# Joining the two directions of a block-wise triangular inversion in one thread, with products that alternate between tiles of the array

## Chip, cores and metric

One NeuronCore of a Trainium2 chip runs the whole program. The metric is the device time of one execution in microseconds (us); lower is better. The time before is 1053.76 us, the median of three runs.

## The reference, cut to what matters

The reference runs two networks one after the other on 256 tokens of width 1024: a first block (a gated delta rule mixer, a layer norm, a mixture of experts with 32 experts, a gate on an embedding) and a second block of two layers. The change touches the mixer alone. Its core solves a unit lower triangular system per head and chunk:

```python
def _gated_delta_rule(q, k, v, beta, g):
    ...
    lhs = eye + jnp.einsum("nbhik,nbhjk->nbhij", kb, k) * decay * (1.0 - eye)
    solve = functools.partial(lax.linalg.triangular_solve, left_side=True, lower=True,
                              unit_diagonal=True)
    u = solve(lhs, v * beta[..., None])
    w = solve(lhs, kb * jnp.exp(gc)[..., None])
    ...
```

The mixer runs it forwards and backwards over the tokens, for 16 value heads. The kernel works with chunks of 128 tokens and inverts the 128x128 matrices: 2 directions x 16 heads x 2 chunks = 64 of them, in two batches of 32.

## The kernel before, in words

The program is written by a planner. Every piece of work is a Python generator (a thread) that yields the engine it wants next ("pe", "act", "dve"), a Wait for events, or an Alloc of buffers. `Sched.run` takes the thread that could start first by an estimate of every engine's clock, with priorities between near ones, and emits its instructions up to its next yield. So the order on each engine is fixed when the program is built, from the prices of `Sched.price` and `Sched.mm` (line 202); on the chip each engine runs its own list in order and semaphores between engines hold back what is not ready. The price of a matmul also depends on a model of the array's clock in `Sched.array` (line 215).

The first stage (class `Gdn`) projects the tokens to queries and keys (`g_qk`), values (`g_v`) and gates (`g_z`), and at its end projects the result back (`g_out`). Weights come in slabs over SP's queue; each slab is either split by ScalarE and VectorE into two parts, for which three fp32r matmuls do, or used as it is in fp32. The projections are in `Gdn.main` (line 1377), at the lowest priority (9): they fill PE wherever the threads of the heads leave room.

The inversion works on two batches `bt` of 32 matrices, each 16 per direction `d`:

- `base` (line 1164) gathers the 32x32 diagonal blocks of the batch, inverts them column by column on VectorE (`columns`, line 1207), transposes the result with two VectorE instructions into `A` and `B`, sets `base_ev`, copies the blocks to the diagonals of `Sm` and `Tm` and sets `diag_ev`.
- `lev` (line 1225) puts larger blocks together. Below, **level 1** is its first group of products (32x32 blocks of the matrix `la` times the small inverses, written to PSUM bank `px`), **level 2** the second (two products per block and matrix, from `Tm` and the small inverse, into banks `pt` and `pS`); they join 32 to 64. **Level 3** (64x64 blocks of `la` times `Tm`) and **level 4** (`Tm` times `Sm`) join 64 to 128. After each level ScalarE and VectorE copy the result from PSUM to `Tm` or `Sm`, and the next level reads it there.
- `solve` (line 1302) waits for both directions (`lev_ev`) and uses the inverses, for each of the four query/key heads of the batch.

`main` spawns `lev` twice per batch, once for each direction, so the two directions are two threads that the planner interleaves with each other and with the projections. Inside a thread, a level sends all 16 products of one pair of blocks to one tile of the array before it goes on to the other pair; where a block lies in the rows and columns is given by `span`. Only level 2 sends two products in turn, which read the same rows and write different columns. After the experts' router, the second stage loads the experts' weights into buffers that the first stage gave back.

Of the kernel before, what the change touches and what calls it, by code (L numbers as in the profile page):

```python
# [11 lines left out]
AF = mybir.ActivationFunctionType  # L12
OP = mybir.AluOpType
# [8 lines left out]
def size(ap):  # L22

    n = 1
    for d in ap.shape[1:]:
        n *= d
    return n
# [10 lines left out]
PRIO = {  # L38
    "decay": [2, 3], "pick": 4, "base": 1, "lev": 1, "solve": 7, "qk": [2, 3], "v": 5, "z": 6,
    "m_turn": 2, "ranks": 1, "gather": 4, "back": 4, "slot_w": 1, "rest": 6, "act_out": 1, "scatter": 3,  # L40
    "m_const": 2, "parts": 1, "router": 3, "norm2": 1, "e_turn": 1, "embed": 7, "e_gates": 1, "gated": 2,
    "e_const": 2, "tokens": 3, "e_head": 3, "e_conv": 3, "window": 0, "e_out": 1, "keys": 1, "normed": 2,
    "copy": 2, "o_head": 2, "o_const": 2, "select": 2, "attend": 3, "o_gate": 1, "queries": 1, "o_out": 1,
    "rms": 1, "rms_turn": 1, "project": 9, "x_split": 3,
}
# [50 lines left out]
def span(ap):  # L96

    n = 0
    for st, k in list(ap.ap)[1:]:
        n += abs(st) * (k - 1)  # L100
    o = ap.offset % max(list(ap.ap)[0][0], 1)
    return ap.name, o, o + n
# [38 lines left out]
class Sched:  # L141
# [60 lines left out]
    def mm(self, out, lhsT, rhs, first, last):  # L202
        self.nc.tensor.matmul(out, lhsT, rhs, start=first, stop=last, skip_group_check=True)  # L203
        n, m = size(rhs), size(lhsT)
        one = lhsT.dtype == F32R
        if n == 512 and m == 32:

            self.array(n, n)
            return
        self.array(max(n, 2 * m) if one else 4 * max(n, m) if n > 64 else 2.4 * n if m < 128 else max(4 * n, 2 * m),  # L210
                   (n if one else 4 * n) * rhs.shape[0] / 128.0, 0.0125 if one else 0.0025)

    TICK = 10.24 / 3
# [661 lines left out]
class Gdn:  # L875
# [346 lines left out]
                        eng.tensor_tensor(t, p2[:, k, 0:k, None].to_broadcast([128, k, n]),  # L1222
                                          R[:, k:k + 1, c:c1].to_broadcast([128, k, n]), op=OP.mult)

    def lev(self, bt, d):

        K, S = self.K, self.S
        v, s, Sm, Tm = S.v, S.s, None, None
        yield Wait(self.base_ev[bt])
        Sm, Tm = self.Sm, self.Tm  # L1230
        s32, t32 = self.AB if d == 0 else self.AB[::-1]
        u = slice(16 * d, 16 * d + 16)

        def lower(i):
            return self.LA[4 * bt + (i % 16) // 4, d][:, (i // 2) % 2, i % 2, 0]

        def span(pr):
            return 64 * pr + 32 * d, 64 * pr + 32 * (1 - d)

        px = yield Alloc("bank", [16, 32])  # L1240
        yield "pe"
        for pr in range(2):
            f, t = span(pr)
            for i in range(16 * d, 16 * d + 16):
                S.mm(px[t:t + 32, i % 16, :], lower(i)[f:f + 32, t:t + 32], t32[f:f + 32, i, :],
                     True, True)
        for pr, e in ((0, "act"), (1, "dve")):
            f, t = span(pr)
            o = Tm[t:t + 32, u, 32 * d:32 * d + 32]
            yield e  # L1250
            if pr:
                v.tensor_copy(o, px[t:t + 32])
            else:
                s.activation(o, px[t:t + 32], AF.Copy)
        S.free(px)
        yield Wait(self.diag_ev[bt])
        pt, pS = yield Alloc("bank", [16, 32], n=2)
        for pr in range(2):
            f, t = span(pr)
            yield "pe"  # L1260
            for i in range(16 * d, 16 * d + 16):
                x = Tm[t:t + 32, i, 32 * d:32 * d + 32]
                st = s32[t:t + 32, i, :]
                S.mm(pt[t:t + 32, i % 16, :], st, x, True, True)
                S.mm(pS[f:f + 32, i % 16, :], x, st, True, True)
        for pr in range(2):
            f, t = span(pr)
            yield "act"
            s.activation(Tm[t:t + 32, u, 32 * d:32 * d + 32], pt[t:t + 32], AF.Copy, scale=-1.0)
            yield "dve"  # L1270
            v.tensor_scalar(Sm[f:f + 32, u, t:t + 32], pS[f:f + 32], -1.0, None, op0=OP.mult)
        S.free(pt, pS)
        f, t = 64 * d, 64 * (1 - d)
        px = yield Alloc("bank", [8, 64], n=2)
        for half in range(2):
            yield "pe"
            for i in range(16 * d + 8 * half, 16 * d + 8 * half + 8):
                S.mm(px[half][t:t + 64, i % 8, :], lower(i)[f:f + 64, t:t + 64], Tm[f:f + 64, i, :], True, True)
        for half, e in ((0, "act"), (1, "dve")):
            o = Tm[t:t + 64, 16 * d + 8 * half:16 * d + 8 * half + 8, :]  # L1280
            yield e
            if half:
                v.tensor_copy(o, px[half][t:t + 64])
            else:
                s.activation(o, px[half][t:t + 64], AF.Copy)
            S.free(px[half])
        pS = yield Alloc("bank", [8, 64], n=2)
        for half in range(2):
            yield "pe"
            for i in range(16 * d + 8 * half, 16 * d + 8 * half + 8):  # L1290
                S.mm(pS[half][f:f + 64, i % 8, :], Tm[t:t + 64, i, :], Sm[t:t + 64, i, t:t + 64], True, True)
        for half, e in ((0, "act"), (1, "dve")):
            o = Sm[f:f + 64, 16 * d + 8 * half:16 * d + 8 * half + 8, t:t + 64]
            yield e
            if half:
                v.tensor_scalar(o, pS[half][f:f + 64], -1.0, None, op0=OP.mult)
            else:
                s.activation(o, pS[half][f:f + 64], AF.Copy, scale=-1.0)
            S.free(pS[half])
        S.set(self.lev_ev[bt][d])  # L1300

    def solve(self, bt, ml):

# [73 lines left out]
    def main(self):  # L1377
        K, S, P = self.K, self.S, self.P
        self.Sm = P.tile([128, 32, 128], F32, name="Sm")
        self.Tm = P.tile([128, 32, 64], F32, name="Tm")  # L1380
        self.V = P.tile([128, 2, 16, 128], F32, name="V")
        self.x = P.tile([128, 8, 256], F32, name="xT")
        S.spawn(self.load(), 0)
        for bt in range(2):
            S.spawn(self.base(bt), PRIO["base"])
            for d in range(2):
                S.spawn(self.lev(bt, d), PRIO["lev"])
            for ml in range(4):
                S.spawn(self.solve(bt, ml), PRIO["solve"])
        yield Wait(*self.x_ev[0:2])  # L1390
        S.spawn(self.clear(), 3)
        x = (self.xh, self.xl, self.x)
        acc = None
        for name, i in GDN_ORDER:
            if name == "g_qk":
                b = yield from K.feature_major(name, x, x_ev=self.xs_ev)
                S.spawn(self.qk_head(i, b), PRIO["qk"][i > 3])
            elif name == "g_v":
                b = yield from K.feature_major(name, x, x_ev=self.xs_ev)
                S.spawn(self.v_pair(i, b), PRIO["v"])  # L1400
            elif name == "g_z":
                if i == GDN_FULL:

                    for n, t in zip(("oh", "ol"), x[0:2]):
                        S.slot_views(n, t.rearrange("p (k a) t -> p k (a t)", a=2))
                z = yield Alloc(("z", "zx"), [512])
                b = yield from K.feature_major(name, x, True, x_ev=self.xs_ev)
                S.spawn(self.z_pair(i, b, z), PRIO["z"])
            else:
                if acc is None:  # L1410
                    acc = yield from K.acc()
                yield Wait(self.z_ev[i])
# [12 lines left out]
        self.entry.start(self.x1)  # L1425
# [1625 lines left out]
```

## Time and profile before

| what | us |
|---|---|
| median of three runs | 1053.76 (1052.91 to 1054.62) |
| the profiled execution | 1055.7 |
| its span, first to last instruction | 1053.9 |
| first inversion, level 1 to the end of level 4 | 121.2 to 158.1 |
| second inversion, the same | 274.9 to 304.9 |
| PE busy | 981.7 |
| mean granted clock of PE | 0.966 |

In a table of stretches each engine has its busy time and, in brackets, how many instructions ran; PEclk is the granted clock, where 1.00 is 2.4 GHz and 0.50 is 1.2 GHz. PEld is the weight load of a matmul. Tile names stand for what an instruction writes and reads: `bank<-t,la` is level 1, `bank<-Tm,t` and `bank<-t,Tm` level 2, `bank<-Tm,la` level 3, `bank<-Sm,Tm` level 4 (all at line 203, where the helper issues every matmul; line 126 is the helper for the other engines). An fp32 product is recorded as two loads and two matmuls.

### The profile page before, as it was taken

The numbers are of one execution on the slowest core, as the hardware profiler recorded it, in microseconds if no ns is written. First come the engines' busy times: TensorE is split into PE (matmuls) and PEld (weight loads), VectorE is DVE, ScalarE is ACT, GpSimd is POOL, SyncE is SP. The second block draws the span as 40 slices with busy tenths as digits, with TensorE's granted clock in tenths as the row PEclk, the third lists the DMA queues.
The fourth block names the chain that finished last, engine by engine and source line by source line (L and its number), as shares of the span: only waits on it lengthen the run. The fifth ranks groups of instructions, "written<-read, shape, count | busy, mean of one in ns | idle before, by whom it ended". The sixth has DMA issues, their size and how long they took to land. (4 is left out here: it accounts for less than half of the span.)

```text
span 1053.9 us, 17204 instructions
## 1 busy us (share of the span) xinstructions
PE 981.7 (93%) x6828; PEld 748.5 (71%) x6828; DVE 621.0 (59%) x1150; ACT 485.4 (46%) x896; POOL 123.6 (12%) x129
## 2 busy tenths in 40 slices
PE   8999989999899968998988779999999999998998
PEld 7788889888688762423211139899999988986886
DVE  7869856699835651121111146688776765677673
ACT  3888464893325331201000135666575443545562
POOL 2133220121000220000000043000000000004230
PEclk9999889999899959999999978999999999999999
DMA  6422411124323977999999954354544454633321
GB/s 217 141 95 86 141 61 41 62 100 136 124 83 123 411 310 288 415 416 410 417 412 414 416 187 146 126 185 160 176 146 159 153 177 172 240 113 99 120 81 41
DMA packets 56680, 205.38 MB, mean 195 GB/s; under 512 B 6416, under 2 KB 6800, under 8 KB 56208
## 3 DMA queue, kind: packets, MB, share of 16 engines
q1 hardware_dynamic: 56304, 204.02, 53.0%
q8 instruction: 55, 0.90, 0.3%
q10 hardware_dynamic: 288, 0.19, 0.1%
q14 instruction: 33, 0.27, 0.1%
HBM read 203.14 MB, written 1.05 MB: 194 GB/s over the span
## 5 line engine op out<-in xcount | busy, mean ns | idle before, releaser
L203 PE MATMUL dbank<-xh,hl 128*128 128x256 f32 x1072 | 216.5, 294 | 0.4 <-DVE t L126 0.4
L203 PEld LDWEIGHTS dbank<-xh,hl 128*128 128x128 f32 x1072 | 173.9, 194 | 7.3 <-issue 4.9
L126 DVE TENSOR_TENSOR hl<-raw,hl 128x1024 fp32r<-128x1024 f32 x107 | 131.5, 1234 | 39.0 <-ACT hl L126 33.2
L203 PE MATMUL dbank<-xl,hl 128*128 128x256 f32 x536 | 152.7, 285 | 0.0
L126 ACT ACTIVATE hl<-raw 128x1024 fp32r<-128x1024 f32 x98 | 103.2, 1056 | 92.2 <-PE dbank L203 58.5
L203 PE MATMUL dbank<-hl,xh 128*128 128x256 f32 (+1 forms) x504 | 116.6, 316 | 2.4 <-ACT xh L126 2.4
L203 PEld LDWEIGHTS dbank<-xl,hl 128*128 128x128 f32 x536 | 103.9, 194 | 3.2 <-issue 3.1
L203 PEld LDWEIGHTS dbank<-hl,xh 128*128 128x128 f32 x504 | 86.6, 197 | 8.8 <-ACT xh L126 3.1
L126 POOL TENSOR_TENSOR hl<-raw,hl 128x1024 fp32r<-128x1024 f32 x16 | 38.6, 2419 | 381.1 <-DMA raw<-in_p_gate 243.0
L203 PE MATMUL dbank<-hl,xl 128*128 128x256 f32 (+1 forms) x252 | 78.4, 311 | 2.3 <-DVE xl L126 2.3
L174 ACT ACT_TABLE_LOAD x53 | 68.0, 1283 | 1.6 <-ACTq L2312 0.7
L203 PE MATMUL dbank<-moe_raw,XG 128*32 128x512 f32 x204 | 56.8, 600 | 6.1 <-DMA moe_raw<-in_m_gu 6.0
L126 DVE SCALAR_TENSOR_TENSOR h<-h,cg,dbank 128x256 f32<-128x256 f32 x8 | 3.8, 480 | 86.8 <-ACT h L126 86.8
L203 PEld LDWEIGHTS dbank<-hl,xl 128*128 128x128 f32 x252 | 49.9, 198 | 4.7 <-DVE xl L126 2.9
L203 PE MATMUL dbank<-xT,raw 128*128 128x256 f32 x240 | 53.0, 379 | 0.1
L126 ACT ACTIVATE h<-dbank 128x256 f32<-128x256 f32 x16 | 6.1, 384 | 96.0 <-PE dbank L203 96.0
L203 PEld LDWEIGHTS dbank<-xT,raw 128*128 128x128 f32 x240 | 45.2, 190 | 6.8 <-issue 1.0
L126 DVE TENSOR_TENSOR x<-x,bank 128x512 f32<-128x512 f32 x28 | 18.6, 685 | 39.1 <-PE bank L203 39.1
L126 DVE TENSOR_TENSOR ys<-dbank,ys 128x512 fp32r<-128x512 f32 x16 | 11.0, 690 | 51.8 <-ACT ys L126 51.8
L203 PEld LDWEIGHTS dbank<-moe_raw,XG 128*32 128x32 f32 x204 | 9.9, 108 | 37.1 <-DMA moe_raw<-in_m_gu 23.7
L126 ACT ACTIVATE ys<-dbank 128x512 fp32r<-128x512 f32 x16 | 9.5, 596 | 48.6 <-PE dbank L203 47.7
L203 PE MATMUL dbank<-hl,yh 128*128 128x512 f32 x96 | 31.1, 396 | 0.0
(454 smaller groups left out, 2116.6 us busy)
## 6 DMA issues: line engine op xcount, KB each, us to landing
moe_raw<-in_m_gu SPq DMA_DIRECT2D x51, 512.0 KB, 10.1
moe_raw_m<-in_m_gu SPq DMA_DIRECT2D x25, 512.0 KB, 10.1
hl<-in_m_gu SPq DMA_DIRECT2D x20, 512.0 KB, 10.0
moe_raw<-in_m_dn SPq DMA_DIRECT2D x19, 512.0 KB, 10.1
raw<-in_m_gu SPq DMA_DIRECT2D x18, 512.0 KB, 10.1
raw<-in_g_qk SPq DMA_DIRECT2D x16, 512.0 KB, 4.6
raw<-in_g_z SPq DMA_DIRECT2D x16, 512.0 KB, 3.9
raw<-in_g_v SPq DMA_DIRECT2D x16, 512.0 KB, 3.8
```

The lines of the kernel that those rows point to most:

```text
L126: r = f(*a, **k)
L174: self.nc.scalar.preload_act_table_set(t)
L203: self.nc.tensor.matmul(out, lhsT, rhs, start=first, stop=last, skip_group_check=True)
```

## The change

`lev` now takes a batch and does both directions. At each level the products go round the tiles of the array: at levels 1 and 2 over the four combinations of pair and direction for each matrix, at levels 3 and 4 over the two directions. Each level is issued in two halves of eight matrices, with a yield to the planner before each. The evictions of a level are threads of their own, with the same instructions on the same engines as before, and the level's thread waits for all of them. Level 1 of both directions shares one bank; at level 2 each direction has one bank for both of its products; at levels 3 and 4 each half of the matrices has one bank for both directions. The planner's price for small products becomes 96 units of the array's clock for 32 moving columns (before 76.8) and 128 for 64 (before 153.6).

```diff
-        self.array(max(n, 2 * m) if one else 4 * max(n, m) if n > 64 else 2.4 * n if m < 128 else max(4 * n, 2 * m),
+        self.array(max(n, 2 * m) if one else 4 * max(n, m) if n > 64 else 2 * max(n, 48) if m < 128 else max(4 * n, 2 * m),
...
-    def lev(self, bt, d):
+    def lev(self, bt):
...
+        def evict(e, o, p, scale=None):
+            yield e
+            if e == "act":
+                s.activation(o, p, AF.Copy, scale=scale or 1.0)
+            elif scale:
+                v.tensor_scalar(o, p, scale, None, op0=OP.mult)
+            else:
+                v.tensor_copy(o, p)
...
+        def span(pr, d):
+            return slice(64 * pr + 32 * d, 64 * pr + 32 * d + 32), slice(64 * pr + 32 - 32 * d, 64 * pr + 64 - 32 * d)
+
+        four = [(pr, d, *span(pr, d)) for d in range(2) for pr in range(2)]
         px = yield Alloc("bank", [16, 32])
...
+        for h in range(2):
+            yield "pe"
+            for i in range(8 * h, 8 * h + 8):
+                for pr, d, f, t in four:
+                    S.mm(px[t, i, :], lower(d, i)[f, t], AB[d][1][f, 16 * d + i, :], True, True)
+        yield Wait(*[S.spawn(evict(("act", "dve")[pr], Tm[t, u[d], 32 * d:32 * d + 32], px[t]), "lev")
+                     for pr, d, f, t in four])
         S.free(px)
         yield Wait(self.diag_ev[bt])
...
+        p = yield Alloc("bank", [16, 32], n=2)
+        for h in range(2):
             yield "pe"
...
+            for i in range(8 * h, 8 * h + 8):
+                for pr, d, f, t in four:
+                    x = Tm[t, 16 * d + i, 32 * d:32 * d + 32]
+                    st = AB[d][0][t, 16 * d + i, :]
+                    S.mm(p[d][t, i, :], st, x, True, True)
+                    S.mm(p[d][f, i, :], x, st, True, True)
+        yield Wait(*[S.spawn(evict(*x, -1.0), "lev") for pr, d, f, t in four
+                     for x in (("act", Tm[t, u[d], 32 * d:32 * d + 32], p[d][t]), ("dve", Sm[f, u[d], t], p[d][f]))])
+        S.free(*p)
+        two = [(d, slice(64 * d, 64 * d + 64), slice(64 - 64 * d, 128 - 64 * d)) for d in range(2)]
+        p = yield Alloc("bank", [8, 64], n=2)
         for half in range(2):
             yield "pe"
...
+            for i in range(8 * half, 8 * half + 8):
+                for d, f, t in two:
+                    S.mm(p[half][t, i % 8, :], lower(d, i)[f, t], Tm[f, 16 * d + i, :], True, True)
+        yield Wait(*[S.spawn(evict(("act", "dve")[half], Tm[t, 16 * d + 8 * half:16 * d + 8 * half + 8, :], p[half][t]),
+                             "lev") for half in range(2) for d, f, t in two])
...
+                for d, f, t in two:
+                    S.mm(p[half][f, i % 8, :], Tm[t, 16 * d + i, :], Sm[t, 16 * d + i, t], True, True)
...
-            for d in range(2):
-                S.spawn(self.lev(bt, d), PRIO["lev"])
+            S.spawn(self.lev(bt), PRIO["lev"])
```

## Rows read from the trace of the kernel before

**Rows 1.** The page: busy time of PE, and its clock in 40 slices.
```profile
PE 981.7 (93%) x6828; PEld 748.5 (71%) x6828; DVE 621.0 (59%) x1150; ACT 485.4 (46%) x896; POOL 123.6 (12%) x129
...
PEclk9999889999899959999999978999999999999999
```

**Rows 2.** The page: the chain that ended last, by engine.
```profile
PE 38%; ACT 2%; DVE 1%; DMA 1%; issue 0%; SPq 0%; ACTq 0%
```

**Rows 3.** Table of stretches: length, busy time and count by engine, PEclk, DMA share, GB/s.
```profile
core 0: us, PE busy (x) PEld busy (x) DVE busy (x) ACT busy (x) POOL busy (x), PEclk, DMA share, GB/s
...
240.00:271.00 31.00, 31.00 (x132) 24.17 (x130) 28.33 (x71) 9.04 (x14) 6.28 (x7) 1.00 0.46 153
271.00:275.00 4.00, 0.37 (x4) 0.10 (x4) 3.97 (x5) 0.00 (x0) 0.00 (x0) 1.00 0.62 200
275.00:305.00 30.00, 30.00 (x545) 24.07 (x545) 17.04 (x31) 8.95 (x13) 0.00 (x0) 0.83 0.25 81
...
420.00:606.00 186.00, 163.93 (x737) 45.58 (x736) 32.15 (x53) 19.81 (x40) 0.00 (x0) 1.00 1.03 414
```

**Rows 4.** Timeline of PE: start, us, tiles, count, [idle before <-releaser].
```profile
135.64 0.21 PE L203 MATMUL bank<-t,Tm 32*32 32x32 f32 x1 [2.28 <-issue]
...
274.90 5.36 PE L203 MATMUL bank<-t,la 32*32 32x32 f32 x128 [3.63 <-DVE t L126]
```

**Rows 5.** Timeline of PE inside level 1: one tile; a change of pair.
```profile
121.19 0.97 PE L203 MATMUL bank<-t,la 32*32 32x32 f32 x25 [2.37 <-DVE t L126]
...
275.52 0.60 PE L203 MATMUL bank<-t,la 32*32 32x32 f32 x17
```

**Rows 6.** Timeline of SP's queue around its pause.
```profile
377.12 2.82 SPq L228 DMA_DIRECT2D moe_raw_m<-in_m_dn  x3
398.87 3.18 SPq L228 DMA_DIRECT2D moe_raw<-in_m_dn  x5
```

**Rows 7.** Groups by line and form on PE: busy us, mean ns | idle before.
```profile
L203 PE MATMUL bank<-t,la 32*32 32x32 f32 x256 | 10.6, 217 | 6.0 <-DVE t L126 6.0
L203 PE MATMUL bank<-Tm,la 64*64 64x64 f32 x128 | 9.8, 242 | 0.0
L203 PE MATMUL bank<-Tm,t 32*32 32x32 f32 x256 | 8.5, 195 | 0.0
L203 PE MATMUL bank<-t,Tm 32*32 32x32 f32 x256 | 8.5, 195 | 2.3 <-issue 2.3
L203 PE MATMUL bank<-Sm,Tm 64*64 64x64 f32 x128 | 8.3, 220 | 0.0
```

**Rows 8.** Timeline of PE inside level 2, across a change of rows.
```profile
286.97 0.19 PE L203 MATMUL bank<-Tm,t 32*32 32x32 f32 x1
...
287.19 0.19 PE L203 MATMUL bank<-Tm,t 32*32 32x32 f32 x1
...
287.22 0.19 PE L203 MATMUL bank<-Tm,t 32*32 32x32 f32 x1
...
287.31 0.19 PE L203 MATMUL bank<-Tm,t 32*32 32x32 f32 x2
...
287.38 0.19 PE L203 MATMUL bank<-Tm,t 32*32 32x32 f32 x1
```

**Rows 9.** Table of stretches around levels and the projections between them.
```profile
126.40:130.90 4.50, 4.50 (x26) 4.43 (x24) 3.65 (x5) 4.31 (x9) 2.25 (x3) 0.62 0.00 0
...
139.80:143.40 3.60, 3.60 (x33) 3.48 (x32) 3.54 (x10) 2.68 (x7) 1.44 (x2) 0.50 0.35 117
...
280.20:286.30 6.10, 6.10 (x18) 4.01 (x16) 3.44 (x5) 2.33 (x3) 0.00 (x0) 0.74 0.26 85
286.30:290.20 3.90, 3.90 (x257) 3.85 (x256) 3.07 (x4) 1.43 (x3) 0.00 (x0) 1.00 0.56 165
290.20:293.80 3.60, 3.60 (x12) 1.18 (x4) 1.38 (x2) 1.17 (x2) 0.00 (x0) 0.53 0.32 123
...
297.40:299.30 1.90, 1.90 (x33) 1.88 (x33) 0.00 (x0) 0.59 (x1) 0.00 (x0) 1.00 0.06 17
```

**Rows 10.** Evictions by tile: ns min/median/max, first and last start, forms.
```profile
L126 DVE TENSOR_SCALAR Sm<-bank x12: 669/686/699, 138.0 to 305.0; 32x512 f32<-32x512 f32 x8, 64x512 f32<-64x512 f32 x4
...
L126 ACT ACTIVATE Tm<-bank x16: 570/588/592, 123.5 to 300.5; 32x512 f32<-32x512 f32 x12, 64x512 f32<-64x512 f32 x4
```

More of the change, by code (lines that the diff above doesn't have):

```diff
@@ L1223, in columns @@
                                           R[:, k:k + 1, c:c1].to_broadcast([128, k, n]), op=OP.mult)
-    def lev(self, bt, d):
+    def lev(self, bt):
         K, S = self.K, self.S
-        v, s, Sm, Tm = S.v, S.s, None, None
+        v, s = S.v, S.s
         yield Wait(self.base_ev[bt])
         Sm, Tm = self.Sm, self.Tm
[L1231 to L1238, printed above, removed]
-        px = yield Alloc("bank", [16, 32])
[L1241 to L1254, printed above, removed]
@@ new lines, in lev, with lower @@
+        AB = self.AB, self.AB[::-1]
+        u = [slice(16 * d, 16 * d + 16) for d in range(2)]
+        def lower(d, i):
+            return self.LA[4 * bt + i // 4, d][:, (i // 2) % 2, i % 2, 0]
+        def evict(e, o, p, scale=None):
[8 more added lines that the diff above has]
+            return slice(64 * pr + 32 * d, 64 * pr + 32 * d + 32), slice(64 * pr + 32 - 32 * d, 64 * pr + 64 - 32 * d)
@@ L1255, in lev @@
         S.free(px)
         yield Wait(self.diag_ev[bt])
-        pt, pS = yield Alloc("bank", [16, 32], n=2)
-        for pr in range(2):
-            f, t = span(pr)
+        p = yield Alloc("bank", [16, 32], n=2)
+        for h in range(2):
             yield "pe"
[L1261 to L1274, printed above, removed]
+            for i in range(8 * h, 8 * h + 8):
[4 more added lines that the diff above has]
+                    S.mm(p[d][f, i, :], x, st, True, True)
@@ L1275, in lev @@
+        yield Wait(*[S.spawn(evict(*x, -1.0), "lev") for pr, d, f, t in four
[3 more added lines that the diff above has]
+        p = yield Alloc("bank", [8, 64], n=2)
         for half in range(2):
             yield "pe"
-            for i in range(16 * d + 8 * half, 16 * d + 8 * half + 8):
-                S.mm(px[half][t:t + 64, i % 8, :], lower(i)[f:f + 64, t:t + 64], Tm[f:f + 64, i, :], True, True)
@@ L1279, in lev @@
[L1279 to L1287, printed above, removed]
+            for i in range(8 * half, 8 * half + 8):
+                for d, f, t in two:
+                    S.mm(p[half][t, i % 8, :], lower(d, i)[f, t], Tm[f, 16 * d + i, :], True, True)
@@ L1288, in lev @@
+        yield Wait(*[S.spawn(evict(("act", "dve")[half], Tm[t, 16 * d + 8 * half:16 * d + 8 * half + 8, :], p[half][t]),
+                             "lev") for half in range(2) for d, f, t in two])
+        S.free(*p)
+        p = yield Alloc("bank", [8, 64], n=2)
         for half in range(2):
             yield "pe"
-            for i in range(16 * d + 8 * half, 16 * d + 8 * half + 8):
-                S.mm(pS[half][f:f + 64, i % 8, :], Tm[t:t + 64, i, :], Sm[t:t + 64, i, t:t + 64], True, True)
@@ L1292, in lev @@
[L1292 to L1300, printed above, removed]
+            for i in range(8 * half, 8 * half + 8):
+                for d, f, t in two:
+                    S.mm(p[half][f, i % 8, :], Tm[t, 16 * d + i, :], Sm[t, 16 * d + i, t], True, True)
@@ L1302, in solve @@
+        yield Wait(*[S.spawn(evict(("act", "dve")[half], Sm[f, 16 * d + 8 * half:16 * d + 8 * half + 8, t], p[half][f],
+                                   -1.0), "lev") for half in range(2) for d, f, t in two])
+        S.free(*p)
+        for d in range(2):
+            S.set(self.lev_ev[bt][d])
     def solve(self, bt, ml):
```

## The prediction

> **What bounds the kernel now.** I began with the page. TensorE (PE) is busy 93% of the span, and its clock row shows full speed except in six slices, three of which lie in the first third and read 8 [rows 1]. The chain that ended last is no help here: it accounts for some 42% of the span, so it stops before it reaches the first stage [rows 2]. I therefore read the stage from a table of stretches [rows 3]. From 240 to 305 us PE is full in every stretch but one; from 271 to 275 it stands nearly idle, and that is the wait of the second inversion for VectorE's base, 3.63 us [rows 4]. The first inversion waits 2.37 us in the same way [rows 5]. ScalarE has room in 240 to 305 us; VectorE has little in 240 to 271 us, 28.33 of 31 [rows 3]. So the first stage is bound by PE, in the order in which its instructions were written out, and whatever PE time the inversion gives back moves the end of the stage.
>
> Does a shift at the end of the first stage reach the end of the kernel? From 420 to 606 us the weights of the experts come in at 414 GB/s and set the pace [rows 3]. But the queue of transfers stands still before that, from a last group of issues at 377.12 us to the next at 398.87 us, because its buffers are full until PE uses them [rows 6]. So PE releases this stage, and it moves with PE, one for one.
>
> **The products of the levels.** Each product is recorded as two pairs of weight load and matmul. Level 1 has 256 records in both inversions and level 2 has 512 under two names that overlap; levels 3 and 4 have 128 each. Their busy time is 10.6 + 8.5 + 9.8 + 8.3 = 37.2 us, counting the two overlapping names of level 2 once [rows 7].
>
> Three speeds are visible. Level 1 sends sixteen products to one tile of the array, and at full clock 25 records span 0.97 us: (0.97 - 0.19)/24 = 32 ns each, where 0.19 us is one matmul [rows 5, 8]. Level 2 alternates already, between two column tiles, and takes 3.9 us for 256 records, 15.2 ns each [rows 9]. Levels 3 and 4 stay on one tile: 32 records in 1.9 us, 59 ns each [rows 9]. So alternation between two tiles halves the price.
>
> The trace doesn't show steady alternation between tiles that differ in rows, which the change uses at every level. It shows its beginning. Where level 1 goes from one pair to the other, rows and columns change together within one bank, and 17 records span 0.60 us, (0.60 - 0.19)/16 = 25.6 ns instead of 32 [rows 5], so about 100 ns were overlapped. Where level 2 changes its rows, 16 records start between 287.22 and 287.38 us, 10 ns each, against 14 records in the 0.22 us before, 15.7 ns [rows 8]. I take the nearest steady row: 15.2 ns for levels 1 and 2, and half of 59 ns for levels 3 and 4. Levels 1 and 2: 768 x 15.2 = 11.7 us; levels 3 and 4: 256 x 29.5 = 7.6 us; together 19.3 us, a saving of **17.9 us**. The best end is 10 ns for the small products: 7.7 + 7.6 = 15.3 us, saving 21.9. The worst end is no overlap between rows, and then the products keep their prices and save nothing.
>
> A rule speaks against it. The Trainium skill, TensorEngine Tiling (Array Packing), Restrictions and Gotchas, says that different row tiles can't access the same PSUM bank at the same time. By that rule the new order, which writes one bank from two or four row tiles, would gain nothing, and the saving would be 0 instead of 17.9; the short overlap within one bank at level 1 leans the other way. The Trainium skill, TensorE: Matmul & The Clock Gate, Part 3, says that a weight load overlaps a running matmul only when its row group differs; by that, level 2 before would not overlap, and the trace disagrees: 15.2 ns against 32.
>
> **The clock.** It falls to the lower level (1.2 GHz) around these small products, and other products pay too. Mean clock is 0.62 in 126.4 to 130.9 us, 0.74 in 280.2 to 286.3 and 0.53 in 290.2 to 293.8, all stretches of ordinary projections [rows 9]. That costs (1 - clock) x length: 1.7 + 1.6 + 1.7 = 5.0 us. Level 3 once runs wholly at 0.50 [rows 9], a loss already in the 9.8 us above. Before each of the first two stretches PE had been idle and then sent single-tile products; before the last it had sent nothing but level 2 for 3.9 us. Afterwards the idle time before level 1 remains, and so does the long run of level 2. I count one fall for each, in both inversions: four, each like the last one, (1 - 0.53) x 3.6 = 1.7 us. They cost 6.8 us and the 5.0 us vanish: **-1.8**. Bounds: no falls, +5.0; six falls, -5.2.
>
> **Waits.** The number of matmuls and evictions is unchanged, and no transfer is added; the cost line prices only products with at most 64 moving columns and a stationary side below 128, which only these levels have [rows 7], so it steers where the planner puts them. What moves is the wait: a level of both directions must be evicted before the next begins. Level 2 has four evictions on each engine, VectorE's 0.69 us each and ScalarE's 0.59 [rows 10], so 2.8 us; levels 1 and 3 have two on each, 1.4 us. That is 5.6 us per inversion, 11.2 in both, in which PE has no product of the inversion. Queued on PE behind the next level are the projections, and the planner must place some ahead of it. Before, each direction covered the other, and projections covered the rest: PE was full in 275 to 305 us [rows 3]. They still exist, so the cover is there; but the planner misjudged the base by 2.37 and 3.63 us [rows 4, 5], and I charge a third of the 11.2: **-3.7 us**; bounds 0 and -11.2. Level 4's last eviction only leads into the solves, as before.
>
> Two costs I leave as they are: the waits for the base, since VectorE's work doesn't change, and the 2.28 us in the middle of the first level 2 in which PE waited for nothing visible [rows 4]. It may go (+2.3) or come once more in each inversion (-4.6).
>
> **The sum:** 17.9 - 1.8 - 3.7 = 12.4 us. The profiled execution took 1055.7 us around its span of 1053.9; 12.4 less is 1043.3. It stands 1.9 us above the median of the three runs, 1053.8, so on the median's scale I forecast **1041.4 us**. The bounds of its small terms give 6 to 18 us, 1036 to 1048.
>
> **Rivals.**
> *VectorE takes the first half back.* VectorE is busy 28.33 of 31 us ahead of the second base [rows 3]. If PE arrives there earlier and finds no projections to put in, it waits longer, and the first inversion's half of the gain is lost: 1053.8 - 6.2 = 1047.6. Against it: output projections were still left after the base.
> *Four tiles overlap and the clock holds.* 21.9 + 5.0 - 3.4 for the falls after the base, less 1.9 for waits: 21.6 us, 1032.2. For it: 10 ns at the change of rows.
> *The change does not do what it says.* The products of different rows into one bank don't overlap. The Trainium skill's rule on row tiles, above, says as much. Products as before, a third of the waits: 1053.8 + 3.7 = 1057.5 if nothing else goes, about 1053.8 if the clock gains what the waits cost.
> *The waits are laid bare (slower).* The planner puts each level straight behind the last, as it put level 1 in front of projections that could have run. PE idles 11.2 us, and the 19.3 us of products run at the lower level, twice as long: 17.9 + 5.0 - 11.2 - 19.3 = -7.6, so 1061.4 at full exposure. It decides from the point where three quarters of the waits and products are so exposed (0.75 x 30.5 = 22.9). Against it: in the kernel before, projections stand between nearly all levels.
>
> **How the numbers follow.** Forecast 0.50; VectorE 0.15; four tiles 0.12; no overlap 0.12, half of it within 0.2% and half slower; bare waits 0.08; the last 0.03 is a planner's reordering elsewhere, within 0.2%. A measurement of this kernel can tell about 0.2%, 2.1 us, from no change. Faster is 0.50 + 0.15 + 0.12 = 0.77; within 0.2% 0.06 + 0.03 = 0.09; slower 0.06 + 0.08 = 0.14. The range runs from 1033 to 1054: it holds the forecast with its bounds, VectorE's case, the no-overlap case at its better end and the near half of the four-tile case; outside are the slower cases and the far half, together 0.20.
>
> **What would show it.** Right: the level products' busy time near 19 us instead of 37.2, with small products at 15 ns or less and 64 x 64 ones near 30 ns; a clock that is lower for one short stretch or two in each inversion; PE full between the levels; the first expert product and the issue of transfers some 12 us earlier than 398.87. Wrong: 32 and 59 ns on alternating tiles; idle PE between levels behind evictions; or a longer wait for VectorE's transposes than 3.63 us, with the first inversion's gain visible before it and gone after.

## The result, and the profile after

The changed kernel took 1035.88 us, the median of four runs (1033.12 to 1037.65), beside 1053.34 us of the kernel before on the same chip: a ratio of 0.983, with a 95% interval of 0.981 to 0.986. The forecast was 1041.4 us with a range of 1033 to 1054. The direction and the range were right; the gain is 17.5 us where 12.4 were forecast.

I read the page first. Two lines answer to [rows 1]:

```profile
PE 955.9 (93%) x6832; PEld 723.2 (70%) x6832; DVE 620.9 (60%) x1142; ACT 485.5 (47%) x902; POOL 131.6 (13%) x138
...
PEclk9999989999899989999999889999999999998999
```

PE is busy 25.8 us less, and the slices that read 8 in the first third are two instead of three. Next the level products, by form, against [rows 7]:

```profile
L203 PE MATMUL bank<-t,Tm 32*32 32x32 f32 x256 | 6.4, 218 | 4.0 <-issue 4.0
L203 PE MATMUL bank<-Tm,t 32*32 32x32 f32 x256 | 6.4, 218 | 2.4 <-DVE Tm L126 2.4
L203 PE MATMUL bank<-Tm,la 64*64 64x64 f32 x128 | 4.5, 221 | 0.0
L203 PE MATMUL bank<-Sm,Tm 64*64 64x64 f32 x128 | 4.2, 220 | 0.0
L203 PE MATMUL bank<-t,la 32*32 32x32 f32 x256 | 3.8, 236 | 6.1 <-DVE t L126 6.1
```

The two names of level 2 overlap and count once, so the sum is 3.8 + 6.4 + 4.5 + 4.2 = 18.9 us; the forecast was 19.3, and the kernel before had 37.2. The mean ns of one matmul hardly moved: a single product is as long as ever, but more of them run at once. Level 2 also shows two kinds of idle time that it had less of before, or none.

The table of stretches of the changed kernel shows the speeds, and what is left between the levels (columns as in [rows 3]):

```profile
122.03:123.89 1.86, 1.86 (x129) 1.80 (x129) 1.86 (x3) 1.86 (x5) 0.26 (x1) 0.50 0.26 97
129.50:130.67 1.17, 1.17 (x138) 1.17 (x139) 0.46 (x1) 1.14 (x4) 0.54 (x2) 1.00 0.05 14
146.21:148.31 2.10, 2.10 (x64) 2.03 (x65) 0.86 (x2) 1.79 (x4) 0.00 (x0) 1.00 0.00 0
...
264.00:269.00 5.00, 1.34 (x35) 0.51 (x37) 4.87 (x7) 1.06 (x1) 0.00 (x0) 0.97 0.62 203
269.00:290.00 21.00, 18.02 (x528) 14.95 (x518) 15.30 (x27) 7.51 (x12) 0.00 (x0) 0.85 0.34 111
290.00:337.00 47.00, 46.98 (x300) 40.30 (x296) 28.63 (x39) 22.25 (x30) 2.54 (x2) 1.00 0.55 212
...
356.30:379.80 23.50, 13.61 (x96) 13.16 (x95) 12.60 (x46) 9.60 (x22) 5.90 (x6) 0.71 0.70 282
```

Level 2 at full clock starts 138 records in 1.17 us, 8.5 ns each, against 15.2 before: its products go round four blocks of rows with two column tiles each, eight tiles in all, where they had two. Level 4 takes 2.10 us for 64 records of 64 columns, 33 ns each with its end counted (29 to 31 from start to start), against 59. Level 1 runs at a clock of 0.50 and takes (1.86 - 0.2)/127 = 13 ns, 0.2 us being one matmul. In 269 to 290 us PE is busy 18.02 of 21 us; before, the second inversion filled PE wholly. The timeline names what came in between (columns as in [rows 4]):

```profile
122.03 1.93 PE L203 MATMUL bank<-t,la 32*32 32x32 f32 x128 [2.42 <-DVE t L126]
...
128.78 0.21 PE L203 MATMUL bank<-Tm,t 32*32 32x32 f32 x1 [0.94 <-DVE Tm L126]
...
129.50 0.21 PE L203 MATMUL bank<-Tm,t 32*32 32x32 f32 x1 [0.46 <-DVE Tm L126]
...
132.86 0.26 PE L203 MATMUL bank<-t,Tm 32*32 32x32 f32 x1 [2.00 <-issue]
...
136.24 2.08 PE L203 MATMUL bank<-t,onesr 128*128 128x512 f32 x2 [2.03 <-ACT t L126]
...
268.59 1.91 PE L203 MATMUL bank<-t,la 32*32 32x32 f32 x128 [3.66 <-DVE t L126]
...
274.89 0.21 PE L203 MATMUL bank<-Tm,t 32*32 32x32 f32 x1 [0.49 <-DVE Tm L126]
...
278.98 0.26 PE L203 MATMUL bank<-t,Tm 32*32 32x32 f32 x1 [2.03 <-issue]
```

The waits for the base are what they were (2.42 and 3.66 us, before 2.37 and 3.63). New are short waits of level 2 for VectorE's evictions of level 1, and a wait of another head's matmul for ScalarE (136.24). The gap "issue" in the middle of level 2, which came once in the kernel before, now comes in each inversion.

SP's queue, which issues the transfers of the weights, ends its pause 17.1 us earlier than in [rows 6]:

```profile
362.06 1.87 SPq L228 DMA_DIRECT2D moe_raw_m<-in_m_dn  x3
381.74 3.00 SPq L228 DMA_DIRECT2D moe_raw<-in_m_dn  x5
```

Every matmul of the trace, put into one of three kinds, gives an account of both inversions together (from 4 us ahead of level 1 to the first solve, and to the last product of level 4):

| us | before | after | difference |
|---|---|---|---|
| level products | 37.0 | 18.8 | -18.2 |
| PE idle | 8.7 | 15.0 | +6.2 |
| other products | 30.6 | 23.4 | -7.2 |
| of these, lost to the lower clock | 7.4 | 5.3 | -2.1 |

The other 5.1 us of other products are projections that stand elsewhere now: the stretches behind the two inversions are 3.5 and 1.5 us longer, clock left aside. Behind the second inversion another 0.8 us of clock loss is gone. So -18.2 + 6.2 - 2.1 - 0.8 = -14.9 us. The last product of the router's first matmuls, which ends the stage, starts at 356.32 instead of 370.40 us: 14.1 earlier, though level 1 began 0.8 later in this run. With these 0.8 us the account closes.

### The profile page after: what moved, and what is told of

Same layout as the page of the kernel before. It is cut to its first block, busy times and chain, and to the rows that moved or that the text cites. A ratio compares the mean times of both kernels' runs of the same rounds, so it can differ in the third digit from the quotient of the medians.

```text
span 1031.3 us, 17216 instructions
## 1 busy us (share of the span) xinstructions
PE 955.9 (93%) x6832; PEld 723.2 (70%) x6832; DVE 620.9 (60%) x1142; ACT 485.5 (47%) x902; POOL 131.6 (13%) x138
## 5 line engine op out<-in xcount | busy, mean ns | idle before, releaser
L126 DVE TENSOR_TENSOR hl<-raw,hl 128x1024 fp32r<-128x1024 f32 x104 | 127.6, 1234 | 36.2 <-ACT hl L126 33.8
L126 POOL TENSOR_TENSOR hl<-raw,hl 128x1024 fp32r<-128x1024 f32 x19 | 45.7, 2410 | 354.0 <-DMA raw<-in_p_gate 235.4
```

What stands on the lines that cost most here:

```text
L126: r = f(*a, **k)
```

## Experiments

Three theories stood first. **A**: the gain is the overlap of alternating products. **B**: it is the merged thread and the new order of the work. **C**: part of it is the planner's other order behind the first stage. The medians below are to be held against 1036 us for the changed kernel and 1053.5 us for the kernel before.

**e0_changed_again**: no edit.

> The changed kernel once more, beside the three that follow, for a second trace of it. Theory A: the end of the first stage (last product of the router's first matmuls) comes again some 14 us earlier than in the kernel before; what lies behind it differs from run to run with where the clock falls, so the router's part may be 3 us longer or shorter than in the first trace: 1033 to 1041 us. Theory C (the later order of the work gives 4 to 5 us of the gain): the stretch from 140 MB of transfers to the end is again 4 us shorter than in the kernel before.

Measured: 1036.35 us, median of five (1035.32 to 1037.22), ratio 0.984 (0.982 to 0.986). The stage ends at 355.61 us, 14.8 earlier than before. The router's stretch, 23.5 us long in the first trace, is this time

```profile
355.60:382.40 26.80, 16.93 (x96) 16.49 (x95) 12.56 (x46) 9.57 (x22) 5.89 (x6) 0.62 0.62 243
```

with the same instructions and a mean clock of 0.62 instead of 0.71; the kernel before had 26.5 us at 0.58. So the 3 us that the first trace gained there are a matter of where the clock happens to fall. From 140 MB of transfers to the end the two traces of the changed kernel have 443.7 and 444.3 us and that of the kernel before 448.2; e2, below, has the order of the kernel before in that stretch and takes 444.6. So the order behind the stage is not what made these 4 us: they lie in the scatter of the one trace of the kernel before, whose execution was 2.2 us above its median. What theory C says of the price line is tested in e3 and e4.

**e1_in_turn**: the same thread and order, one tile after the other.

```diff
-            for i in range(8 * h, 8 * h + 8):
-                for pr, d, f, t in four:
+            for pr, d, f, t in four:
+                for i in range(8 * h, 8 * h + 8):
...
-                for d, f, t in two:
+            for d, f, t in two:
+                for i in range(8 * half, 8 * half + 8):
```

> The changed kernel with one thing undone: within each half of a level the products go to one tile after the other (eight of a tile, then the next), as in the kernel before; the merged thread, the price line, the order of every other instruction on every engine stay. Theory A (the gain is the overlap of alternating products): level 1 goes back to 32 ns a record at full clock, level 2 to about 15, levels 3 and 4 to 59, so the products take some 37 us of TensorE again instead of 18.9; some of the idle time between the levels (about 9 us over both inversions) is filled by them, so 12 to 18 us are lost: 1048 to 1054 us. Theory B (the merged thread and the new order of the work give the gain): within 4 us of the changed kernel, 1033 to 1040 us.

Measured: 1043.79 us, median of six, ratio 0.992 (0.990 to 0.995). 7.7 us are lost: less than A said, more than B. The groups by form:

```profile
L203 PE MATMUL bank<-t,la 32*32 32x32 f32 x256 | 9.3, 216 | 6.0 <-DVE t L126 6.0
L203 PE MATMUL bank<-Tm,t 32*32 32x32 f32 x256 | 8.4, 202 | 0.0
L203 PE MATMUL bank<-t,Tm 32*32 32x32 f32 x256 | 8.4, 202 | 1.3 <-issue 1.3
L203 PE MATMUL bank<-Tm,la 64*64 64x64 f32 x128 | 6.8, 221 | 0.0
L203 PE MATMUL bank<-Sm,Tm 64*64 64x64 f32 x128 | 6.8, 221 | 0.0
```

The products take 31.3 us, 12.4 more than alternating, and not 37: with eight products to a tile the changes of tile come more often than in the kernel before, and each one overlaps a little (51 ns a record at levels 3 and 4, where 59 were expected). And half of the idle time goes: no wait for VectorE at level 2, one "issue" gap of 1.3 us; PE is idle 7.3 us instead of 15.0. The lower clock costs the other products 9.2 us instead of 5.3. 12.4 - 7.7 + 3.9 = 8.6; the stage ends 8.0 us later than in the changed kernel. Outside the level products the order on every engine is that of the changed kernel. So going from eight in turn to full alternation is worth 12 us of PE time, of which about 8 reach the end.

The other 9.9 us of the gain stay: the run is that far below the 1053.65 us of the kernel before beside it. Against the account of the kernel before, 5.8 us of level products are saved, since changing tile after eight products is a coarse alternation, and 1.4 us of idle time, but the clock costs 1.8 us more; the stage ends 6.0 us earlier (364.36 against 370.40). What the merged thread is worth with no overlap at all was not run, so theory B is bounded by this and not refuted.

**e2_two_threads**: alternation inside each direction alone, on the kernel before.

```diff
-        for pr in range(2):
-            f, t = span(pr)
-            for i in range(16 * d, 16 * d + 16):
+        for i in range(16 * d, 16 * d + 16):
+            for pr in range(2):
+                f, t = span(pr)
...
-        for pr in range(2):
-            f, t = span(pr)
+        for h in range(2):
             yield "pe"
-            for i in range(16 * d, 16 * d + 16):
+            for i, (f, t) in [(i, span(pr)) for i in range(16 * d + 8 * h, 16 * d + 8 * h + 8) for pr in range(2)]:
```

> The kernel before, with its two threads and its price, but inside each direction the products alternate between the two pairs at levels 1 and 2 (two tiles at level 1, four at level 2); levels 3 and 4 have one tile in one direction and stay. Nothing else moves on any engine. Theory A: level 1 goes from 32 to about 15 ns a record (256 records, 4 us), level 2 from 15.2 to between 8.5 and 10 (512 records, 3 us); with a microsecond or two given back in gaps, 1046 to 1049 us. Theory B: 1052 to 1055 us, as before.

Measured: 1048.85 us, median of twelve, but 1045.8 to 1058.2 apart; ratio 0.998 (0.995 to 1.001). That is no proof of a gain. The trace shows what stood against one: level 2 fell to between 8.5 and 8.7 ns a record at full clock, on four tiles, and level 1 of the first inversion to 15, on two, as A has it; but level 1 of the second inversion ran at a clock of 0.50 and took 25 ns, and then the second inversion's levels 3 and 4 ran almost throughout at half clock.

```profile
292.30:305.80 13.50, 13.50 (x103) 12.21 (x102) 3.29 (x4) 1.77 (x3) 0.00 (x0) 0.50 0.07 19
```

In [rows 9] a stretch of the same products, with the same order around it, has a clock of 1.00. The stage ended at 371.7 us, no earlier than before. The price per product is confirmed; the gain in time is open.

**e5_l34_in_turn**: only levels 3 and 4 in turn (the last two hunks of e1).

> The changed kernel with the 64 x 64 products of levels 3 and 4 in turn (eight of one direction, then eight of the other), levels 1 and 2 still alternating, every other instruction in the same order. Theory A: 256 records go from 30 to 59 ns, 7.5 us lost: 1041 to 1045 us. Theory B, or a wait that hides these products: 1035 to 1038 us.

Measured: 1041.64 us, median of six, ratio 0.991 (0.988 to 0.993); 5.5 us lost, as A expected.

```profile
L203 PE MATMUL bank<-Tm,la 64*64 64x64 f32 x128 | 6.8, 221 | 0.0
L203 PE MATMUL bank<-Sm,Tm 64*64 64x64 f32 x128 | 6.8, 221 | 0.0
```

The two groups take 13.6 us instead of 8.7, 4.9 more, and the stage ends 4.3 and 5.0 us later than in the two traces of the changed kernel. At these levels nearly all of the price reaches the end. Only the order of these products differs from the changed kernel, on all engines, and PE is idle 14.1 us in the inversions, hardly less than 15.0: little was waiting to fill the time.

**e3_price_alone** and **e4_old_price**: the price line alone, on the kernel before and taken out of the changed one.

```diff
-... 2.4 * n if m < 128 ...
+... 2 * max(n, 48) if m < 128 ...
```

> The kernel before with the changed price line alone: the planner books 0.0800 + 0.0025 us for a small product at the lower clock instead of 0.064 and 0.128 us (32 and 64 columns), and so places other work otherwise. Theory A: this is noise of the order, 1050 to 1056 us. Theory C (part of the measured 17 us is the planner's other order behind the first stage): 1047 to 1050 us, with the stage's end where it was and the gain after it.

> The changed kernel with the price line of the kernel before (0.064 and 0.128 us a product at the lower clock where the change books 0.080). Theory A: the products cost what they cost, whatever the planner books: 1034 to 1042 us, the products again near 19 us busy. Theory C (the planner's new price is what places the work well): the gaps between the levels grow by 3 us or more, 1040 to 1046 us.

Measured: e3 1052.53 us, median of twelve (1049.65 to 1061.54), ratio 1.000 (0.998 to 1.002): the price gains nothing there. e4 1040.54 us, median of six, ratio 0.988 (0.986 to 0.990): 4 us slower than the changed kernel. PE is idle 16.2 us in the inversions instead of 15.0, not 3 us more, and the stage ends at 356.00 us, as in the changed kernel. Between 140 and 150 MB of transfers, where no level product is left, it loses 3.5 us against e0. The order of the instructions behind the stage is another in e4, so the price acts here through the order that the planner finds much later; about 4 of the 17 us hang on that, and whether by the truer price or by chance these two runs can't say.

**e6_spread**: projections forced between the parts of level 2.

```diff
-        for h in range(2):
+        for h in range(4):
+            if h:
+                S.cur.last, S.cur.end = S.cur.last + 1.5, (None, 0.0)
             yield "pe"
-            for i in range(8 * h, 8 * h + 8):
+            for i in range(4 * h, 4 * h + 4):
```

> The changed kernel with level 2 cut into four parts instead of two, and 1.5 us of planned time kept free ahead of the second, third and fourth, so that projections go between them. Theory F (the gaps of 2.0 to 2.3 us in and behind level 2, in which TensorE waits for nothing visible, are its own instructions coming in more slowly than products of 8.5 ns use them up): with projections between, these gaps shrink from 6.5 us over both inversions to under 3, and the kernel gains 2 to 4 us: 1032 to 1034 us. Rival G (the gaps belong to the products themselves, their banks or semaphores): the gaps stay, and the kernel is within 2 us of the changed one or slower by the later end of the level.

Measured: 1043.76 us, median of six, ratio 0.990 (0.988 to 0.993): slower than the changed kernel. (The 6.5 us of that text counted in the wait for ScalarE at 136.24, which is no gap of this kind; 4.0 us are.) No "issue" gap is left inside level 2 in either inversion, as F said; one of 2.17 us stands behind the level, at 142.97 us, ahead of a matmul with an identity (`bank<-identr,t`), with no packet of instructions (last section) in the 6 us before it. But the plan around the level got worse:

```profile
135.12 0.55 PE L203 MATMUL dbank<-xh,hl 128*128 128x256 f32 x1 [4.32 <-DVE raw L126]
...
275.47 1.74 PE L203 MATMUL bank<-t,la 32*32 32x32 f32 x128 [3.66 <-DVE t L126]
```

The projection put into the gap waits 4.32 us for its operand, and the second base is done 6.7 us later (275.47 against 268.7). Inside level 2 the run bears F out, but its forecast of a gain failed.

**e7_diag_later**: the copies to the diagonals as a thread of their own, at a later priority, and their event waited for ahead of level 3.

```diff
-        yield Wait(self.diag_ev[bt])
         p = yield Alloc("bank", [16, 32], n=2)
...
+        yield Wait(self.diag_ev[bt])
         two = [(d, slice(64 * d, 64 * d + 64), slice(64 - 64 * d, 128 - 64 * d)) for d in range(2)]
```

> The changed kernel with the sixteen copies of the diagonal blocks put behind level 1's evictions in priority, and their event waited for ahead of level 3 instead of level 2, which reads only level 1's results. Theory H (level 2's waits, 0.94, 0.46, 0.49 and 0.46 us, are for evictions that queue behind these copies on VectorE): 1.4 to 2.4 us less, 1033 to 1036 us. Rival: the copies are then late for level 3 and the wait only moves there: as the changed kernel or up to 2 us slower.

Measured: 1041.89 us, median of six, ratio 0.990 (0.987 to 0.992). A miss, and no test of H: in the second inversion the planner still put fifteen of the copies in front of level 1's evictions on VectorE, and level 2 waited longer.

```profile
275.79 1.93 PE L203 MATMUL bank<-t,la 32*32 32x32 f32 x128 [4.68 <-DVE t L126]
...
282.34 0.26 PE L203 MATMUL bank<-Tm,t 32*32 32x32 f32 x1 [1.76 <-ACT Tm L126]
```

**e8_pair**: level 2 by pair, TensorE's order alone.

```diff
-            for i in range(8 * h, 8 * h + 8):
-                for pr, d, f, t in four:
+            for i in range(16):
+                for pr, d, f, t in four[h::2]:
                     x = Tm[t, 16 * d + i, 32 * d:32 * d + 32]
```

> The changed kernel with level 2's products ordered by pair: the first half of the level takes the four tiles of the first pair (all sixteen products of each), the second half those of the second pair; the changed kernel takes eight products of all. Four tiles alternate as before. Only TensorE's order inside level 2 changes; the order on every other engine is the same. The first half then needs only ScalarE's evictions of level 1 and the second only VectorE's. Theory H: level 2's four waits for VectorE (2.35 us over both inversions) shrink to what is left when the second half comes up 1.1 us later: 1 to 2 us gained, 1034 to 1035.5 us, with the gaps of 2 us inside level 2 where they were in the count of TensorE's instructions. Rival: these waits are covered by something that comes due later, and the time stays within 0.7 us of 1036.1.

Measured: 1034.53 us, median of six (1032.81 to 1035.83), ratio 0.981 (0.978 to 0.983): inside the expectation, but its interval meets that of e0. The timeline does not bear H out:

```profile
121.59 1.29 PE L203 MATMUL bank<-t,la 32*32 32x32 f32 x128 [2.36 <-DVE t L126]
...
127.36 0.21 PE L203 MATMUL bank<-Tm,t 32*32 32x32 f32 x1 [1.42 <-ACT Tm L126]
...
131.44 0.26 PE L203 MATMUL bank<-t,Tm 32*32 32x32 f32 x1 [1.39 <-issue]
...
282.73 2.08 PE L203 MATMUL bank<-Tm,la 64*64 64x64 f32 x62 [1.64 <-ACT Tm L126]
```

In the first inversion the waits for VectorE became waits for ScalarE, which is no less late (1.42 and 0.36 us); in the second the waits inside level 2 are gone and one of 1.64 us ahead of level 3 took their place. Together they are 3.4 us, where the changed kernel had 2.35. PE is idle 15.0 us, as in the changed kernel, so the 1.5 us of gain, if it is one, does not come from fewer waits. (The changed kernel's level 2 goes round eight tiles and this one round four; at full clock both take 8.5 ns a record. Level 1 met the full clock in this run: (1.29 - 0.2)/127 = 8.6 ns a record, four tiles into one bank.)

**e9_pair_price**: e8, and the planner books what the products took.

```diff
-... 2 * max(n, 48) if m < 128 ...
+... n * n / 32 if m < 128 ...
```

> As the run before, and the price line books what the products took here: 32 cycles for 32 columns (0.029 us a product at the lower clock, measured 0.027) and 128 for 64 columns (0.109, measured 0.107), instead of 96 and 128. If a truer price places the rest better, 1031 to 1034 us; if the plan's order behind is chance, as the price runs so far suggest, anywhere from 1033 to 1041 us.

Measured: 1031.57 us, median of six (1027.89 to 1034.97), ratio 0.978 (0.975 to 0.981): the fastest of all, 4.5 us below the changed kernel. PE is idle 13.2 us in the inversions, level 2 has no wait for an eviction left, and the stage ends at 352.42 us.

```profile
131.09 0.21 PE L203 MATMUL bank<-t,Tm 32*32 32x32 f32 x1 [1.84 <-issue]
...
282.00 2.08 PE L203 MATMUL bank<-Tm,la 64*64 64x64 f32 x62 [0.66 <-ACT Tm L126]
```

Whether the truer price or luck in the order did it is not told apart: e4 moved as far the other way.

**e10_pair_spread**: e8 with level 2 in eight parts and 0.15 us planned ahead of each.

```diff
-        for h in range(2):
+        for h in range(8):
+            if h:
+                S.cur.last, S.cur.end = S.cur.last + 0.15, (None, 0.0)
             yield "pe"
-            for i in range(8 * h, 8 * h + 8):
-                for pr, d, f, t in four:
+            for i in range(4 * (h % 4), 4 * (h % 4) + 4):
+                for pr, d, f, t in four[h // 4::2]:
```

> The order by pair, with level 2 in eight parts and 0.15 us of planned time kept free ahead of each, so that single groups of projections can go between them (a gentler form of the earlier try with 1.5 us). Theory F: the gaps in level 2 in which TensorE waits for its own instructions shrink by the time that projections fill, 1 to 3 us off the first stage's end against the changed kernel; the plan behind may move by a few us either way: 1031 to 1039 us. Rival G: the gaps stay at 2 us.

Measured: 1037.29 us, median of six, ratio 0.984 (0.982 to 0.987). In the second inversion projections stand between all eight parts; 512 weight loads and matmuls of level 2 go by without one "issue" gap, which is F's claim. But the level now lasts from 276.4 to 292.1 us, and the solves that wait for it came later. In the first inversion the planner found little to put in, and the gap stayed:

```profile
131.86 0.25 PE L203 MATMUL bank<-t,Tm 32*32 32x32 f32 x1 [2.27 <-issue]
```

**e11_repeat**: level 1's products twice, straight behind each other, the second time into the same places.

```diff
+        for i in range(16):
+            for pr, d, f, t in four:
+                S.nc.tensor.matmul(px[t, i, :], lower(d, i)[f, t], AB[d][1][f, 16 * d + i, :], start=True, stop=True,
+                                   skip_group_check=True)
```

> The changed kernel with level 1's 64 products issued a second time right behind the first (the same values into the same places, nothing booked by the planner, the order on the other engines unchanged): 128 matmuls and 128 weight loads more of TensorE in each inversion. Theory F (TensorE waits when it has used up the instructions that have come in, at fixed places in its count): the gaps of the first inversion stay ahead of the same counted instructions as in the changed kernel, 1964 and 2174 matmuls and weight loads from the kernel's start, though other products stand there now, and a third stall appears where the dense run is longer; more is lost than the repeated products' own 1.7 us in each inversion: 3.4 to 8 us in all, 1039.5 to 1044 us. Rival G (the gap belongs to a product, its bank or a semaphore): it stays with its product, 256 instructions later in the count, and the loss is 2 to 3.4 us.

Measured: 1038.61 us, median of four, ratio 0.984 (0.982 to 0.987), 2.5 us slower than the changed kernel; the stage ended 4.6 and 5.3 us later than in its two traces.

```profile
125.37 0.37 PE L1259 MATMUL bank<-t,la 32*32 32x32 f32 x10 [2.39 <-issue]
...
135.45 0.21 PE L203 MATMUL bank<-t,Tm 32*32 32x32 f32 x1 [2.57 <-issue]
...
273.32 0.39 PE L1259 MATMUL bank<-t,la 32*32 32x32 f32 x12 [1.80 <-issue]
```

By medians F missed the size (2.5 us where 3.4 to 8 were expected), and in the first inversion it missed the place of level 2's stall: that moved 256 instructions on, behind the 2220th, with its product, as G said. But the new stall of 2.39 us among the repeated products of level 1 stands behind the 1708th instruction, and 1708, 1964 and 2220 are 256 apart: the run added just one such step, so here the two theories look alike. The second inversion tells them apart. There the stall of 1.80 us stands behind the 4506th instruction, the same count as in both traces of the changed kernel (the gap at 278.98 us in the first). In those it was ahead of a product of level 2; in e11, with the repeats of both inversions pushing level 2 back, it is ahead of a repeated product of level 1. That is F's claim, and G does not give it. Level 2's product keeps 0.41 us, 512 instructions further on.

## Why the prediction was right, and where its terms were off

**What bounds the stage: right.** PE time given back moved the end of the stage and then the transfers (14.1 and 14.8 us at the router, 17.1 and 14.5 at the end of SP's pause, in the first trace and in e0).

**The products: right in sum, 18.3 us where 17.9 were forecast.** The two prices were each a little off, in opposite directions, and that the sum came so close is luck. Levels 1 and 2 took 10.2 us, not 11.7: the nearest steady row, two column tiles at 15.2 ns, was too dear, and four or eight tiles give 8.5 at full clock; but level 1 ran at half clock, 13 ns, and the rest of level 2 behind its gaps too, 10.6 ns on eight tiles at a clock of 0.50. Levels 3 and 4 took 8.7, not 7.6, the end of each group counted. The rival without overlap between rows in one bank is refuted: level 1 writes one bank from four row tiles, at 32 ns a record in turn and 8.6 alternating (e8). By the Trainium skill's rule (TensorEngine Tiling (Array Packing), Restrictions and Gotchas) it would have stayed at 32; the trace does not agree. Here each tile writes partitions of its own in that bank; tiles that write the same ones were not run. That the price comes from the alternation is shown by e5 and e1, in which it alone was undone. Of the gain in time e1 took back 7.7 us of 17.5; the rest is put down to the coarse alternation that is left in e1, to less idle time and to the part behind the stage by the account alone.

**The clock: the wrong sign.** The step "four falls of 1.7 us, and 5.0 us vanish: -1.8" counted only three stretches of the kernel before. Over both inversions and the stretch behind them its lower clock cost other products 7.4 + 0.8 = 8.2 us, and the changed kernel 5.3: +2.9, a term mis-sized by 4.7 us, most of it in what the kernel before lost (8.2, not 5.0). The changed kernel lost 5.3 and 5.0 us in its two traces; of the kernel before there is one. e2 shows the same term going the other way: levels 1 and 2 at half their price or little more, and the clock at 0.50 for most of the 13.5 us behind them; its stage ended no earlier than before.

**The waits: too small, and put in the wrong place.** I charged 3.7 us for evictions that lie bare between levels. PE was idle 6.2 us more, and the sign "PE full between the levels" was not met. Of this 2.35 us are evictions, all ahead of level 2; levels 3 and 4 were covered. 2.1 us more are waits of other products for late operands from ScalarE. That PE reaches them sooner than the planner booked may be the reason but is not shown: in e9, with the prices as measured, a wait of 3.65 us for VectorE stands in that place. 1.75 us are the "issue" gap, 2.28 us once before and 2.0 us in each inversion now: of the possibility named as "once more in each inversion", two gaps more, one came.

**The rest.** 18.3 + 2.9 - 6.2 = 15.0 us at the end of the stage (measured: 14.1 and 14.8), against 12.4: the clock gave 4.7 us more than forecast and the waits took 2.5 us more, so the errors partly cancel. The medians differ by 17.2 to 17.5; the 2.4 us behind the stage are not explained. From the stage's end to the kernel's end the kernel before has 683.5 us, the longest of all fourteen traces, and the changed kernel 675.0 and 679.0; e2, with the order of the kernel before there, has 676.0. So the 2.4 us lie within what one trace differs from the next, and no run here separates them. The forecast's bounds of 6 to 18 us do not follow from its terms: the bounds it gives for clock and waits make 4.9 to 19.2 us one at a time, and 1.5 to 22.9 together.

**The rivals.** VectorE took back part of the first half: the first batch's solves began 9.8 us earlier than before, the second batch's level 1 only 6.3, because VectorE's two transposes ahead of it started 6.3 us earlier (264.74 against 271.08) and no more. In between PE worked 3.5 us longer on projections that had stood inside the inversions, so the difference was not lost. The waits were not laid bare as a whole: 2.35 of 11.2 us of evictions were. Four tiles did overlap, as that rival had it, but the clock did not hold: level 1 ran at 0.50.

## What to carry to other kernels

Small products that go to different tiles of the array in turn cost a fraction of the same products sent to one tile: at full clock 8.5 ns a record on four tiles or eight, 15 on two, 32 on one, and 30 instead of 59 for 64x64. Eight tiles paid only at the lower clock: 10.6 ns (level 2 of the changed kernel, behind its gaps) against 13 to 13.5 on four (its level 1, and level 2 of e8). When PE time shrinks this much, look at once for what was hidden behind it: here a third of 18 us came back as waits for evictions, late operands and instructions. If an order is planned from prices, try the price of what was made faster as measured (e4 and e9 point that way, e3 does not), and expect a few us either way from any such change by chance.

## What was not expected of the hardware

PE can run out of instructions. The gaps marked "issue" inside dense runs stood in the first inversion behind the same counted instruction, the 1964th weight load or matmul of the kernel, in both traces of the changed kernel, in the kernel before and in e1 to e5 and e7 to e10, though the order of the products there was not the same. In e11 they stood behind the 1708th, the 2220th and, as in the changed kernel, the 4506th. The page has a queue for instructions,

```profile
q8 instruction: 55, 0.90, 0.3%
```

55 packets of 16 KB for 13,664 matmuls and weight loads, one for about 250. The page does not name the engine; that they are TensorE's is read from this count. In each of these gaps a packet had started 2.3 to 3.0 us before PE went on (130.43 and 132.86 us in the changed kernel). At 8.5 ns for a load and a matmul together, 256 instructions are used up in 1.1 us. That supply and gap belong together is shown by these times and counts, by e11 and by e10's second inversion; the supply itself could not be changed, so its own speed is left open.
